# A two-layer hybrid encoder on one core: unread state products left out, and six loads of each feed-forward block given a place in the queue

## The chip, the cores and the metric

The kernel runs on one NeuronCore of a Trainium2 chip, as one program with one launch. The metric is the device time of that program in microseconds (us), lower is better. Five engines work beside each other, each from a queue of its own in a fixed order: TensorE (PE in the profile; its weight loads are PEld) multiplies matrices, VectorE (DVE) and ScalarE (ACT) work on elements, GpSimd (POOL) does some of that and issues DMAs, and SyncE (SP) issues most DMAs. All DMAs run on 16 shared DMA engines.

## The reference

The input is `x` (1024 tokens of 1024 values) and a memory of 256 tokens. `DEPTH` is 2, so there are two layers. Layer 0 mixes tokens with windowed attention, layer 1 with a two-directional gated recurrence; each mixer also has four cross-attention heads into the memory. Each layer ends with a feed-forward block. Cut to what matters here:

```python
h = x
for layer in range(2):
    u = rmsnorm(h, norm_g[layer, 0])
    y = mixer(u)                                   # 0: window attention, 1: recurrence
    h = h + rmsnorm(y, norm_g[layer, 1])
    f = conv_ffn(rmsnorm(h, norm_g[layer, 2]))     # gelu(conv(v @ w_gate)) * (v @ w_up) @ w_out
    h = h + rmsnorm(f, norm_g[layer, 3])

def step(state, inp):                              # the recurrence, one chunk of tokens
    qd, ke, vc, dec = inp
    o = qd @ state                                 # what earlier chunks give to this one
    state = dec * state + ke.T @ vc                # the state that the next chunk reads
    return state, o
```

The scan starts from a zero state and runs once over the tokens and once over the reversed tokens. The state after the last chunk of either scan is returned by the scan and used by nobody. The last `rmsnorm` of a layer has the weight `norm_g[layer, 3]`, and the first one of the next layer has `norm_g[layer + 1, 0]`.

## The kernel before

All products are float32 accurate: each operand is split into a high and a low part (`wh`, `wl`; `uh`, `ul`), and TensorE does three passes, high by high, high by low, low by high. The split is an ACT cast (L86, L76, L599) and a DVE subtraction (L87, L77, L600). The queues of all engines are written by a planner: it goes through the program with a model of the durations and puts each instruction into its engine's queue when, by its plan, the operands and a free buffer are there. A load with a free buffer therefore goes out as early as its buffer exists, however far back in the program it stands. `tc.issue_after(ins)` adds one rule: what is traced in the block on the engine of `ins` stands behind `ins` in that queue; it does not wait for `ins` to finish.

**The feed-forward block, `ffn(l, ...)`.** Its second half multiplies the 22 hidden tiles with `ffn_w_out` by a seven-product scheme (two by two blocks, seven instead of eight products). `SECOND = (1, 6, 7, 4, 2, 5, 3)` is the order of the seven products, called k below; each runs over p = 0 to 10, so there are 77 units (k, p). `unit(k, p)` loads two halves of one staging tile `st`, the weights (L891, from the input, or from `w2s`, sums of weight blocks made earlier in DRAM) and the hidden values (L892, `hid`), 256 KB each, and splits them. Staging has four buffers, the ring of split operands four. `second_ahead()` keeps up to three units made ahead of the one that TensorE works on. One unit is 12 matmuls of 128x512 (L575).

Around the units stand these loads, all on SP:

- `grow` (L104): one row of `norm_g` copied to all 128 partitions, 512 KB: `g3`, and in layer 0 also `g0`. Half of `g3` is then negated by DVE (L922). GpSimd first uses `g3` in `scaled`, after product 4 (L958).
- `rows(b, t)` (L935): 128 tokens of `h1d`, the layer's residual, 512 KB. The first four are for the token half `ia`: in the program they stand inside product 5, at p = 1, 3, 5 and 7, as the last argument of `tail`. `tail` adds the normed result to the row (DVE, L946), and SP stores it (L950). The tile `x` has four buffers in layer 0 and two in layer 1.

**The recurrence, `hgrn()`.** Eight heads; for each, `head` calls `direction` for the two scans d and the two token halves b in the order (0, 0), (1, 1), (0, 1), (1, 0). One call covers four chunks of 128 tokens. It ends with: `ER *= k` (DVE, L1237), four transposes of `ER` (PE, L1247), a copy of them to `kT` (ACT, L1249), four products `pu` of `kT` with the values (PE, L1252), and then the states `S`, one after another: `nx` is the chunk that reads the new state, and

```python
                if not 0 <= nx < NT:
                    continue
```

leaves out the state that no chunk reads. Its transpose and product were done by then. Which chunk that is: the last of the forward scan (d = 0, b = 1, c = 3) and the first of the backward scan (d = 1, b = 0, c = 0), so two of the sixteen chunks of each head. Between the directions stand the projections of the same and the next head (L81 to L83, the bulk of TensorE's work here) and the cross-attention units.

Of the kernel before, what the change touches and what calls it, by code (L numbers as in the profile page):

```python
# [8 lines left out]
F32 = mybir.dt.float32  # L9
# [4 lines left out]
ALU = mybir.AluOpType  # L14
# [4 lines left out]
P = 128  # L19
T = 1024  # L20
D = 1024
NT = T // P
# [25 lines left out]
def build(tc, A, out):  # L48
    nc = tc.nc
    act, dve, pool, pe = nc.scalar, nc.vector, nc.gpsimd, nc.tensor  # L50
# [34 lines left out]
    def split(h, l, src):  # L85
        act.copy(h, src)  # L86
        dve.tensor_tensor(l, src, h.bitcast(F32), op=ALU.subtract)  # L87
# [14 lines left out]
    def grow(pl, src_row, name):  # L102
        g = pl.tile([P, D], F32, tag=name, bufs=1, name=name)
        nc.sync.dma_start(g, src_row.to_broadcast([P, D]))  # L104
        return g
# [327 lines left out]
    class Out:  # L433
# [66 lines left out]
        def rows(self, wp, t):  # L500
            x = wp.tile([P, D], F32, tag="x", bufs=2, name="x")
            nc.sync.dma_start(x, self.src[t * P:(t + 1) * P, :])
            return x
# [75 lines left out]
    def ffn(l, wo, dst, gnext, halves_, out_halves):  # L579
# [10 lines left out]
        i, j = halves_  # L590
# [6 lines left out]
        def nsplit(h, l_, src):  # L597

            act.activation(h, src, AF.Copy, scale=-1.0)  # L599
            dve.scalar_tensor_tensor(l_, src, -1.0, h.bitcast(F32), op0=ALU.mult, op1=ALU.subtract)  # L600
# [119 lines left out]
        hd = dram.tile([8, NP2, P, 512], F32, name=f"hid{l}")  # L720
# [162 lines left out]
        SECOND = (1, 6, 7, 4, 2, 5, 3)  # L883
        where = {1: (2, None), 2: (3, None), 4: (1, None), 5: (None, 0), 7: (None, 1), 6: (None, 2), 3: (None, 3)}
        todo = [(k, p) for k in SECOND for p in range(NP2)]
        made = []

        def unit(k, p):
            r = stg.tile([P, 2, 512], F32, tag="st", name="st")
            a_, d_ = where[k]  # L890
            nc.sync.dma_start(r[:, 0, :], A["ffw2"][l, p, a_] if d_ is None else w2d[p][d_])  # L891
            nc.sync.dma_start(r[:, 1, :], hd[k, p])  # L892
            pl = hold_pool if k == 3 and 0 <= p - (NP2 - LAST[l]) < HOLD[l] else ring
            h, l_ = [pl.tile([P, 1024], F32R, tag=t, name=t) for t in ("wh", "wl")]
            r = r.rearrange("p a b -> p (a b)")
            if k == 6:
                nsplit(h[:, :512], l_[:, :512], r[:, :512])
                split(h[:, 512:], l_[:, 512:], r[:, 512:])
            else:
                split(h, l_, r)  # L900
            return h, l_

        def second_ahead():
            if todo and len(made) < (LAST[l] if todo[0][0] == 3 else 3):
                made.append(unit(*todo.pop(0)))
# [10 lines left out]
        np_ = tc.alloc_tile_pool(name=f"fn{l}", bufs=2, reuse_waits="tile")  # L916
        hold_pool = tc.alloc_tile_pool(name=f"fh{l}", bufs=HOLD[l], reuse_waits="tile")
        if gnext:
            tc.keep_in_program_order(act.preload_act_table_set("natural_log_exp_and_others"))
        g3 = grow(np_, A["norm_g"][l, 3:4, :], "g3")  # L920
        g0 = grow(np_, A["norm_g"][l + 1, 0:1, :], "g0") if gnext else None
        dve.tensor_scalar_mul(g3[:, 512:], g3[:, 512:], -1.0)  # L922
        y = {q: yp.tile([P, 4, 512], F32, name=q) for q in ("c11", "c21", "c12", "c22")}
        ss = {q: yp.tile([P, 4], F32, name=q) for q in ("q11", "q21", "q22")}
        left = lambda: {t: psl.tile([P, 512], F32, tag=f"x{t}", name="X") for t in (2, 3, 0, 1)}
# [3 lines left out]
        def rows(b, t):  # L929

            if gnext or b == ia:
                x = np_.tile([P, D], F32, tag="x", bufs=4 if gnext else 2, name="x")
            else:
                x = stg.tile([P, D], F32, tag="st", name="st")
            nc.sync.dma_start(x, h1d[l][tok(b, t), :])  # L935
            return x

        def tail(b, t, ya, sa, yb, sb, x):

            ts_ = tok(b, t)  # L940
            sq = np_.tile([P, 1], F32, tag="sq", name="sq")
            dve.tensor_tensor(sq, sa, sb, op=ALU.add)
            rs = rstd_of(np_, sq, 1, D, "p")
            last = not gnext and b == out_halves[1] and t == 3
            for c, yy in ((slice(0, 512), ya), (slice(512, 1024), yb)):
                dve.scalar_tensor_tensor(x[:, c], yy, rs[:, 0:1], x[:, c], op0=ALU.mult, op1=ALU.add)  # L946
                if last:
                    (nc.sync if c.start == 0 else act).dma_start(dst[ts_, c], x[:, c])
            if not last:
                nc.sync.dma_start(dst[ts_, :], x)  # L950
            if gnext:
                norm_T(np_, pst, x, g0, uh, ul, 4 * b + t)
# [12 lines left out]
        ia, ib = out_halves  # L965
        D0, D1 = slice(0, 512), slice(512, 1024)
        pst = None
        for k in SECOND:
            if k == 5:
                Xs = left()  # L970
            ps = Vs if k == 2 else Xs
            hold = []
            for p in range(NP2):
                while len(made) < 1:
                    second_ahead()
                h, l_ = made.pop(0)
                second_ahead()
                if k == 3 and p >= NP2 - LAST[l]:
                    hold.append((p, h, l_))
                else:  # L980
                    mms(k, p, h, l_, ps, range(4), k in (1, 5, 2) and p == 0)
                if k == 5 and p in (1, 3, 5, 7):
                    t = p // 2
                    tail(ia, t, y["c11"][:, t, :], ss["q11"][:, t:t + 1], y["c21"][:, t, :], ss["q21"][:, t:t + 1], rows(ia, t))
            if k == 3:
                last = [rows(ib, t) for t in range(4)]
            for t in range(4):
                if k in (1, 6, 7, 4):
                    act.copy(y[{1: "c11", 6: "c12", 7: "c22", 4: "c21"}[k]][:, t, :], ps[t])  # L989
                elif k in (2, 5):  # L990
                    q = y[{2: "c11", 5: "c22"}[k]][:, t, :]
                    dve.tensor_tensor(q, ps[t], q, op=ALU.add)  # L992
                else:
                    for p, h, l_ in hold:
                        mms(k, p, h, l_, ps, (t,), False)
                    sb = np_.tile([P, 1], F32, tag="sb", bufs=1, name="sb")
                    y1 = np_.tile([P, 512], F32, tag="y1", name="y1")
                    dve.tensor_tensor(y1, ps[t], y["c12"][:, t, :], op=ALU.add)  # L998
                    sumsq(np_, y1, sb)
                    y2 = np_.tile([P, 512], F32, tag="y2", bufs=1, name="y2")  # L1000
                    dve.tensor_tensor(y2, y1, g3[:, D0], op=ALU.mult)
                    tail(ib, t, y2, sb, y["c22"][:, t, :], ss["q22"][:, t:t + 1], last[t])
            if k == 4:
                scaled("c21", "q21", D1)
            elif k == 5:
                scaled("c22", "q22", D1)
            elif k == 2:
                scaled("c11", "q11", D0)
                psr.release()
                if gnext:  # L1010
                    pst = tc.alloc_tile_pool(name=f"fnps{l}", bufs=2, space=PSUM, side="right", reuse_waits="tile")
# [8 lines left out]
    def hgrn():  # L1020
        l = 1
        eq = tc.alloc_tile_pool(name="hgq", bufs=1, reuse_waits="tile")
        es = tc.alloc_tile_pool(name="hgs", bufs=1, reuse_waits="tile")
        early = tc.alloc_tile_pool(name="hg0", bufs=1, reuse_waits="tile")
# [126 lines left out]
        def direction(h, r, d, b, qin, S, As):  # L1151

            q, k = r["q"][b], r["s"][d][b]
# [25 lines left out]
            ER = early.tile([P, 512], F32, tag="ER", bufs=2, name="ER")  # L1179
# [54 lines left out]
            pool.tensor_copy(dec.unsqueeze(2), EP.rearrange("p (c t) -> p c t", t=P)[:, :, e:e + 1])  # L1234
            bs = slice(b * 512, (b + 1) * 512)
            sum_steps[1].send(pool.tensor_tensor(qin[:, bs], EP, q, op=ALU.mult))
            dve.tensor_tensor(ER, ER, k, op=ALU.mult)  # L1237
            dve.copy_predicated(Az[d], gm[d], pa.rearrange("p c t -> p (c t)"))
            a2 = lambda x: x.rearrange("p c t -> p (c t)")
            if As[b] is None:  # L1240
# [2 lines left out]
            else:  # L1243
                pool.tensor_tensor(a2(As[b]), a2(As[b]), Az[d], op=ALU.add)
            tp = bank("pt")
            for c in range(4):
                pe.transpose(tp[:, c, :], ER[:, c * P:(c + 1) * P], ident)  # L1247
            kT = wp.tile([P, 4, P], F32, tag="kT", bufs=1, name="kT")
            act.copy(kT, tp)  # L1249
            pu = bank("pu")  # L1250
            for c in range(4):
                pe.matmul(pu[:, c, :], kT[:, c, :], r["v"][:, 4 * b + c, :], start=True, stop=True)  # L1252
            for c in (range(3, -1, -1) if d else range(4)):
                cg = 4 * b + c
                nx = cg - 1 if d else cg + 1
                if not 0 <= nx < NT:
                    continue
                if cg == (NT - 1 if d else 0):
                    act.copy(S[:, nx, :], pu[:, c, :])
                else:  # L1260
                    dve.scalar_tensor_tensor(S[:, nx, :], S[:, cg, :], dec[:, c:c + 1], pu[:, c, :],
                                             op0=ALU.mult, op1=ALU.add)
# [300 lines left out]
```

## Time and profile before

| | before |
|---|---|
| median of 3 runs | 2662.06 us (2660.34 to 2668.28) |
| profiled execution, first to last instruction | 2663.0 us; the page gives no other time for it |
| PE busy | 2605.1 us, 98% |
| DVE, ACT, POOL busy | 1820.8 us, 1377.3 us, 468.3 us |
| second half of layer 0's feed-forward block, from its first jam of loads to its last unit | about 1005 to 1215 us |
| the recurrence | about 1245 to 1905 us |
| second half of layer 1's feed-forward block | about 2440 to 2660 us |

Matmuls overlap in these records: a 128x512 one is shown with 0.39 us, while the next one starts 0.227 us after it. How long a stretch of TensorE's work takes is therefore read from the starts, not from the durations. In the views in windows the columns after the engines are the granted TensorE clock (1.00 is full speed), the busy share of the DMA engines, and GB/s.

### The profile page before, as it was taken

What the parts mean: (1) busy time and instruction counts of PE and PEld (TensorE: products, weight loads), DVE (VectorE), ACT (ScalarE), POOL (GpSimd) and SP (SyncE); (2) the same over time, 40 slices, a digit from 0 to 9 for tenths busy, and PEclk for the clock granted to TensorE, in tenths of its full rate; (3) what the DMA queues carried; (4) which work ended last, traced back from release to release, by engine and by line L of the source; (5) the groups of instructions that cost most, each with busy time, mean ns of one, the idle gap of its engine ahead of it and who ended that gap; (6) DMA issues with size and microseconds to landing.
All of it is one profiled execution on the core that took longest, in us unless ns stands there. A gap on an engine that the chain in (4) does not pass through costs nothing. (4 is left out here: it accounts for less than half of the span.)

```text
span 2663.0 us, 39112 instructions
## 1 busy us (share of the span) xinstructions
PE 2605.1 (98%) x14420; PEld 2186.3 (82%) x14420; DVE 1820.8 (68%) x3043; ACT 1377.3 (52%) x2503; POOL 468.3 (18%) x520
## 2 busy tenths in 40 slices
PE   8999999999999999999999999999999999999998
PEld 7888887788888887887888888888887788888887
DVE  6778886578655565478688686887757755656447
ACT  6467676545444444455455554555534444444453
POOL 0321010211111100031224131231311111110013
PEclk9999999999999999999999999999999999999999
DMA  9772222367787857574235351103437778785666
GB/s 354 248 169 58 74 89 82 104 188 196 197 203 192 209 153 250 190 246 160 85 110 147 83 127 55 52 25 101 139 103 198 191 194 209 197 204 167 220 194 233
DMA packets 195728, 425.93 MB, mean 160 GB/s; under 512 B 20048, under 2 KB 56272, under 8 KB 189904
## 3 DMA queue, kind: packets, MB, share of 16 engines
q1 hardware_dynamic: 161552, 324.06, 37.6%
q0 software_dynamic: 24544, 90.19, 16.3%
q10 hardware_dynamic: 9440, 9.19, 1.1%
q8 instruction: 113, 1.85, 0.3%
q14 instruction: 79, 0.65, 0.1%
HBM read 330.04 MB, written 116.39 MB: 168 GB/s over the span
## 5 line engine op out<-in xcount | busy, mean ns | idle before, releaser
L87 DVE TENSOR_TENSOR wl<-st,wh 128x1024 fp32r<-128x1024 f32 (+1 forms) x238 | 263.4, 1113 | 318.4 <-ACT wh L86 308.1
L86 ACT CAST wh<-st 128x1024 fp32r<-128x1024 f32 (+1 forms) x238 | 222.5, 937 | 289.7 <-PE X L575 187.8
L81 PE MATMUL pj<-uh,wh 128*128 128x512 f32 x512 | 202.9, 397 | 4.0 <-DVE q L1118 2.0
L575 PE MATMUL X<-wl,wh 128*128 128x512 f32 x528 | 205.4, 391 | 0.3 <-DVE wl L87 0.3
L575 PE MATMUL X<-wh,wl 128*128 128x512 f32 x528 | 205.0, 390 | 0.0
L575 PE MATMUL X<-wh 128*128 128x512 f32 x528 | 199.6, 391 | 2.6 <-ACT c L989 2.1
L82 PE MATMUL pj<-ul,wh 128*128 128x512 f32 x512 | 201.7, 394 | 0.1
L83 PE MATMUL pj<-uh,wl 128*128 128x512 f32 x512 | 201.8, 394 | 0.0
L81 PE MATMUL pj<-wh,uh 128*128 128x384 f32 (+1 forms) x512 | 190.3, 373 | 4.7 <-DVE gs L1104 2.5
L83 PE MATMUL pj<-wh,ul 128*128 128x384 f32 (+1 forms) x512 | 187.7, 367 | 0.0
L82 PE MATMUL pj<-wl,uh 128*128 128x384 f32 (+1 forms) x512 | 187.3, 366 | 0.1
L77 DVE TENSOR_TENSOR wl<-st,wh 128x1024 fp32r<-128x1024 f32 (+1 forms) x91 | 116.3, 1283 | 26.0 <-ACT wh L76 25.3
L575 PE MATMUL V<-uh,wh 128*128 128x512 f32 x336 | 130.7, 389 | 0.0
L575 PE MATMUL V<-ul,wh 128*128 128x512 f32 x336 | 130.7, 389 | 0.0
L575 PE MATMUL V<-uh,wl 128*128 128x512 f32 x336 | 130.7, 389 | 0.0
L76 ACT CAST wh<-st 128x1024 fp32r<-128x1024 f32 (+1 forms) x97 | 97.7, 1013 | 44.9 <-PE pj L82 25.2
L575 PEld LDWEIGHTS X<-wh 128*128 128x128 f32 x528 | 99.5, 188 | 24.1 <-ACT c L989 2.5
L575 PEld LDWEIGHTS X<-wl,wh 128*128 128x128 f32 x528 | 99.6, 189 | 21.3 <-DVE wl L87 0.7
L575 PEld LDWEIGHTS X<-wh,wl 128*128 128x128 f32 x528 | 99.5, 188 | 20.7
L81 PEld LDWEIGHTS pj<-uh,wh 128*128 128x128 f32 x512 | 96.3, 188 | 24.2 <-DVE q L1118 3.1
L83 PEld LDWEIGHTS pj<-uh,wl 128*128 128x128 f32 x512 | 96.2, 188 | 18.6
L82 PEld LDWEIGHTS pj<-ul,wh 128*128 128x128 f32 x512 | 96.3, 188 | 18.6 <-DVE ul L87 0.4
(413 smaller groups left out, 7167.9 us busy)
## 6 DMA issues: line engine op xcount, KB each, us to landing
st<-hid SPq DMA_DIRECT2D x154, 256.0 KB, 3.0
st<-in_ffw_dram SPq DMA_DIRECT2D x108, 256.0 KB, 3.4
w2s<-in_ffw_dram POOLq DMA_DIRECT2D x24, 1024.0 KB, 8.4
st<-in_ffw_dram SPq DMA_DIRECT2D x46, 512.0 KB, 4.3
hid<-tt SPq DMA_DIRECT2D x88, 256.0 KB, 4.7
st<-w2s SPq DMA_DIRECT2D x88, 256.0 KB, 3.4
sx<-in_ffw_dram SPq DMA_DIRECT2D x84, 256.0 KB, 4.0
sy<-in_ffw_dram SPq DMA_DIRECT2D x42, 512.0 KB, 6.6
```

Of the source, the lines that this page charges most:

```text
L76: act.copy(h[:, :n], raw)
L77: (eng or dve).tensor_tensor(l[:, :n], raw, h[:, :n].bitcast(F32), op=ALU.subtract)
L81: pe.matmul(o, ah, bh, start=first, stop=False)
L82: pe.matmul(o, ah, bl, start=False, stop=False)
L83: return pe.matmul(o, al, bh, start=False, stop=last)
L86: act.copy(h, src)
L87: dve.tensor_tensor(l, src, h.bitcast(F32), op=ALU.subtract)
L575: last = pe.matmul(o, x, y, start=new, stop=e, skip_group_check=not first)
```

## The change

Two edits. In `direction`, only the chunks whose state is read (`used`, three of four in the two calls above) are multiplied, transposed, copied and multiplied with the values. In `ffn`, the tiles of `g3` and `g0` are still made at the head of the second half, but their loads are issued by `gain(0)` and `gain(1)` behind the hidden-value loads of units (7, 2) and (7, 6), and the rows 0 to 3 of the half `ia` behind those of units (4, 5), (4, 8), (5, 0) and (5, 3).

```diff
@@ unit @@
-            nc.sync.dma_start(r[:, 1, :], hd[k, p])
+            loads[k, p] = nc.sync.dma_start(r[:, 1, :], hd[k, p])
@@ ffn, head of the second half @@
-        g3 = grow(np_, A["norm_g"][l, 3:4, :], "g3")
-        g0 = grow(np_, A["norm_g"][l + 1, 0:1, :], "g0") if gnext else None
-        dve.tensor_scalar_mul(g3[:, 512:], g3[:, 512:], -1.0)
+        gains = [np_.tile([P, D], F32, tag=x, bufs=1, name=x) for x in (("g3", "g0") if gnext else ("g3",))]
+        g3, g0 = gains[0], gains[-1]
+
+        def gain(i):
+
+            nc.sync.dma_start(gains[i], A["norm_g"][l + i, 3 * (1 - i):3 * (1 - i) + 1, :].to_broadcast([P, D]))
+            if i == 0:
+                dve.tensor_scalar_mul(g3[:, 512:], g3[:, 512:], -1.0)
@@ ffn, the units @@
+        due, early = ([(4, 5), (4, 8), (5, 0), (5, 3)], [])
...
                 h, l_ = made.pop(0)
                 second_ahead()
+                if k == 7 and p in (2, 6) and p // 4 < len(gains):
+                    with tc.issue_after(loads[k, p].ins):
+                        gain(p // 4)
+                if k in (4, 5) and (k, p) in due:
+                    with tc.issue_after(loads[k, p].ins):
+                        early.append(rows(ia, due.index((k, p))))
...
-                    tail(ia, t, y["c11"][:, t, :], ss["q11"][:, t:t + 1], y["c21"][:, t, :], ss["q21"][:, t:t + 1], rows(ia, t))
+                    tail(ia, t, y["c11"][:, t, :], ss["q11"][:, t:t + 1], y["c21"][:, t, :], ss["q21"][:, t:t + 1], early[t])
@@ direction @@
-            dve.tensor_tensor(ER, ER, k, op=ALU.mult)
+            used = [c for c in range(4) if 4 * b + c != (0 if d else NT - 1)]
+            us_ = slice(used[0] * P, (used[-1] + 1) * P)
+            dve.tensor_tensor(ER[:, us_], ER[:, us_], k[:, us_], op=ALU.mult)
...
-            for c in range(4):
+            for c in used:
                 pe.transpose(tp[:, c, :], ER[:, c * P:(c + 1) * P], ident)
             kT = wp.tile([P, 4, P], F32, tag="kT", bufs=1, name="kT")
-            act.copy(kT, tp)
+            cs_ = slice(used[0], used[-1] + 1)
+            act.copy(kT[:, cs_], tp[:, cs_])
             pu = bank("pu")
-            for c in range(4):
+            for c in used:
                 pe.matmul(pu[:, c, :], kT[:, c, :], r["v"][:, 4 * b + c, :], start=True, stop=True)
-            for c in (range(3, -1, -1) if d else range(4)):
+            for c in (used[::-1] if d else used):
                 cg = 4 * b + c
                 nx = cg - 1 if d else cg + 1
-                if not 0 <= nx < NT:
-                    continue
```

More of the change, by code (lines that the diff above doesn't have):

```diff
@@ L885, in ffn @@
         todo = [(k, p) for k in SECOND for p in range(NP2)]
-        made = []
+        made, loads = [], {}
         def unit(k, p):
```

## The prediction, as written before the change was run

> **What bounds the kernel now.** I read the page's busy shares first, then windows over the stages, then TensorE's timeline wherever a window showed lost time, and last SP's queue and the waits at that place.
>
> ```profile
> span 2663.0 us, 39112 instructions
> PE 2605.1 (98%) x14420; PEld 2186.3 (82%) x14420; DVE 1820.8 (68%) x3043; ACT 1377.3 (52%) x2503; POOL 468.3 (18%) x520
> ```
>
> TensorE is busy for 98% of the span, so only two things shorten the run: less work for TensorE, or less of the 2663.0 − 2605.1 = 58 us of idling and slow clock. The change has one part of each kind. Windows over the second half of layer 0's feed-forward block (columns: time of PE, PEld, DVE, ACT, POOL, then clock, DMA share, GB/s):
>
> ```profile
> 1014.00:1024.00 10.00, 10.00 (x46) 8.29 (x45) 3.44 (x4) 3.43 (x4) 0.00 (x0) 1.00 1.00 356
> 1024.00:1034.00 10.00, 7.88 (x33) 6.16 (x32) 4.17 (x7) 4.75 (x10) 0.00 (x0) 0.93 0.97 373
> 1034.00:1044.00 10.00, 10.00 (x42) 8.19 (x41) 4.27 (x8) 4.72 (x9) 0.00 (x0) 0.90 0.34 113
> 1054.00:1064.00 10.00, 10.00 (x46) 8.29 (x45) 4.97 (x5) 5.07 (x8) 0.00 (x0) 1.00 0.63 204
> ```
>
> A usual stretch is the last one: 46 matmuls in 10 us, DMA engines 63% busy at 204 GB/s. From 1014 to 1034 the DMA engines are full, then TensorE gets only 33 and 42 matmuls, at a granted clock of 0.93 and 0.90. TensorE's timeline there, and two short windows:
>
> ```profile
> 1029.57 0.39 PE L575 MATMUL X<-wh 128*128 128x512 f32 x1
> 1029.80 0.39 PE L575 MATMUL X<-wl,wh 128*128 128x512 f32 x1
> 1030.02 0.39 PE L575 MATMUL X<-wh,wl 128*128 128x512 f32 x1
> 1032.53 0.80 PE L575 MATMUL X<-wh 128*128 128x512 f32 x1 [2.12 <-ACT c L989]
> ...
> 1036.03 0.39 PE L575 MATMUL X<-wh,wl 128*128 128x512 f32 x1
> ...
> 1032.00:1034.00 2.00, 1.47 (x4) 1.19 (x5) 1.18 (x2) 2.00 (x6) 0.00 (x0) 0.63 0.65 239
> 1034.00:1036.00 2.00, 2.00 (x6) 1.61 (x5) 1.19 (x3) 1.49 (x3) 0.00 (x0) 0.52 0.25 83
> ```
>
> Undisturbed, a matmul starts 0.22 to 0.23 us after the one before it; I use 0.227. The step from 1030.02 to 1032.53 is 2.51, so 2.28 us are lost waiting. The next 8 matmuls take 1036.03 − 1032.53 = 3.50 instead of 1.82 us, because the clock is about half: 1.68 lost. Together **4.0 us**. Who is late stands in SP's queue and in the waits between 1010 and 1035 (total, times, longest):
>
> ```profile
> 1013.67 0.95 SPq L104 DMA_DIRECT2D g<-in_norm_g_dram  x2
> 1015.65 1.18 SPq L935 DMA_DIRECT2D x<-h1d  x2
> 1021.82 1.51 SPq L935 DMA_DIRECT2D x<-h1d  x2
> ...
> ACT wh L599 <- DMA st<-w2s: 8.4, 3, 3.1
> DVE g L922 <- DMA g<-in_norm_g_dram: 5.3, 1, 5.3
> ```
>
> Both norm weights and four rows go out within 9 us, 6 x 512 KB = 3.15 MB, among the loads of the first units of product 6. ACT then waits three times for those weights, and TensorE runs dry once. The record names ACT's copy at L989 as what TensorE waited for; that copy stood behind a cast that waited for its load.
>
> **The change part by part.**
>
> *Loads in layer 0.* At 356 to 373 GB/s, 3.15 MB are 8.6 us of full DMA; three units of look-ahead are 3 x 12 x 0.227 = 8.2 us, and cast and subtraction need part of it. So the burst is just too long, by about the 2.28 us seen. Alone, 0.52 MB delays a unit's load by 1.4 us, and each 2.72 us unit leaves 37% of the DMA time free, 1.0 us: two units take the backlog off again. The six new places are at least three units apart. So the stall goes and I take **−4.0 us**; ends: 0 (the stall only moves) and −4.0 (all that is lost here). The trace has a smaller case, layer 1, with one weight and two rows:
>
> ```profile
> 2458.40 0.41 SPq L104 DMA_DIRECT2D g<-in_norm_g_dram  x1
> ...
> 2459.84 1.39 SPq L935 DMA_DIRECT2D x<-h1d  x2
> ...
> 2457.00:2467.00 10.00, 10.00 (x46) 8.28 (x45) 4.69 (x5) 3.45 (x4) 0.00 (x0) 1.00 1.00 352
> 2467.00:2477.00 10.00, 10.00 (x46) 8.29 (x45) 5.24 (x9) 6.25 (x12) 0.00 (x0) 1.00 0.87 314
> ```
>
> Half the burst, 1.57 MB or 4.3 us of full DMA, with 46 matmuls in both windows: covered. In layer 1 the move is worth **0**; the cover is the same look-ahead.
>
> The rule in the Trainium skill's "TensorE: Matmul & The Clock Gate", section "Why this matters for your kernels", is to leave no idle gap over some 3 us, since a window of idling halves the clock. By that rule the 2.3 us gap here should not have touched the clock, the slow stretch would have another cause and stay, and the sum would lose 1.7 us; in the trace the clock falls in the very window in which the gap ends.
>
> *Are the late loads late for their readers?* Old places of the units they now follow, first readers of the rows, and landing times of these row loads:
>
> ```profile
> 1052.74 0.32 SPq L891 DMA_DIRECT2D st<-w2s  x1
> 1145.58 0.32 SPq L891 DMA_DIRECT2D st<-w2s  x1
> ...
> 1168.61 1.41 DVE L946 SCALAR_TENSOR_TENSOR x<-c,prs,x 128x512 f32<-128x512 f32 x2
> ...
> DMA to landing us min/median/max: 4.2/5.7/10.4
> ```
>
> By the count of loads in SP's queue, 1052.74 is unit (7, 2) and 1145.58 is (5, 3). The last row moves to about 1146 and is read at 1168.61: 23 us, more than the worst landing. `g3` is first read after product 4, later still. DVE's negation of `g3` blocks the subtractions behind it until the load lands: 5.3 us before, in the jam; after, at most that, and under 8.2 us of look-ahead. Cost 0. GpSimd's queue carries none of these loads.
>
> *Third and fourth row of layer 1.* Tile `x` has two buffers there, so these two still cannot start before a stored row is out, wherever the program asks for them:
>
> ```profile
> 2607.49 0.32 SPq L935 DMA_DIRECT2D x<-h1d  x1
> 2610.91 0.32 SPq L935 DMA_DIRECT2D x<-h1d  x1
> SPq L935 <- DMA out_dram<-x: 1.7, 2, 1.2
> PE X L575 <- DVE c L992: 0.5, 1, 0.5
> PE X L575 <- DVE wl L87: 0.3, 1, 0.3
> ```
>
> SP waits 1.7 us for the stores, the unit loads behind it are late, and TensorE loses 0.5 + 0.3 us around 2624 and 2636. The store is on SP too, so a load placed right behind it could hold SP for one landing, some 4 us; ends: −0.8 and +2; I take 0.
>
> *Recurrence.* Removed: 8 heads x 2 chunks = 16 transposes and 16 products; a product is two matmul instructions. Timeline of one place, two group rows (count, busy us, mean ns), and the stage's sum row:
>
> ```profile
> 1282.84 0.60 PE L1252 MATMUL pu<-v,kT 128*128 128x128 f32 x4
> 1283.28 0.60 PE L1247 MATMUL pt<-ident,ER 128*128 128x128 f32 x4
> 1283.72 0.39 PE L1252 MATMUL pu<-v,kT 128*128 128x128 f32 x2
> ...
> L1237 DVE TENSOR_TENSOR ER<-ER,s 128x512 f32<-128x512 f32 x32 | 21.8, 681 | 0.0
> L1249 ACT COPY kT<-pt 128x512 f32<-128x512 f32 x32 | 18.7, 584 | 2.2 <-PE pt L1247 2.2
> ...
> sum 660.00, PE 650.43 PEld 549.02 DVE 512.92 ACT 350.44 POOL 173.19; mean PE 92.92 PEld 78.43 DVE 73.27 ACT 50.06 POOL 24.74
> PE pa L1201 <- POOL E L1216: 2.7, 4, 1.6
> PE pj L81 <- DVE gs L1104: 2.5, 4, 0.8
> ```
>
> Four of either take 0.44 us from start to start, 0.11 each: 16 x (2 + 1) x 0.11 = 5.3 us of TensorE's time. DVE's product and ACT's copy shrink by a quarter 16 times, at most 16 x 0.17 = 2.7 and 16 x 0.15 = 2.3 us; TensorE covers both, so 0. How much of 5.3 comes through? TensorE is busy 650.43 of the stage's 660.00 us. Ends: 0 (each saving falls into a wait for another engine) and 5.3 + 9.6 (the waits vanish too). The stage is 98.5% busy, so I take 0.985 x 5.3 = **−5.2 us**.
>
> *Sum.* 2663.0 − 4.0 − 5.2 = 2653.8 for an execution like the profiled one. The median of the runs is 2662.06, 0.9 lower, so **2652.9 us** for the median.
>
> **The rivals.**
>
> *The clock dip is not the wait's doing* and shows up again: 2652.9 + 1.7 = 2654.6. For it, a wait as long at the start of layer 1's block left the clock at full speed; against it, the coincidence above.
>
> ```profile
> PE Y L575 <- ACT wh L76: 2.2, 1, 2.2
> ...
> 2022.00:2026.00 4.00, 2.78 (x11) 1.83 (x12) 3.59 (x6) 1.90 (x3) 0.00 (x0) 1.00 0.57 126
> ```
>
> *The mixer's part is absorbed.* TensorE reaches the block products (`pa`) or the next projection sooner and waits there longer; the last two rows above are such waits, 5.2 us together. If half to all of 5.3 is lost so: 2655.5 to 2658.1. Against it: 98.5% busy.
>
> *The loads do harm at their new places, or the stall moves.* Price 4.0, time 2656.9. Against it: slack of 1.0 us in each unit, and layer 1's free 1.57 MB. The Trainium skill's "DMA: Bandwidth & Descriptors", section "Rules for kernel authors", advises to issue a DMA early and wait late; by that rule holding these loads back gains nothing, which is this rival's time. The trace disagrees: issued early, they made the weights late.
>
> *Slower: the planner reorders the recurrence.* Shorter directions shift its plan, and TensorE's queue may hold the `pa` products too early, before GpSimd's E is ready. Now that costs 2.7 us at 4 of 32 directions, 0.68 each. At 13 more directions the whole gain of 9.2 is gone (2662); at all 32, 28 x 0.68 = 19 is added: 2672, slower by 0.4%. For it: PE's queue is fixed by a plan that knows no real landing times. Against it: only 3 of 4 steps shrink slightly, in half the calls.
>
> *Better than the sum.* DVE's 2.7 us come before TensorE's waits, and the stage's 9.6 us and layer 1's 0.8 us of waits shrink by half: 2648.
>
> **How the numbers follow.** Forecast 0.46; clock dip stays 0.08; mixer's part absorbed 0.15; loads do harm 0.11; planner 0.10, of it 0.07 beyond 2670; better 0.10. A measurement of this kernel tells about 0.3%, 8 us, from no change: faster means under 2654.1. The forecast has about 2.5 us of scatter from a rewritten plan, so 0.65 of its 0.46 lie below that (0.30), all of the better case (0.10), and 0.03 each of the clock and absorbed cases: faster 0.46, same 0.47, slower 0.07. The range takes in the better case's 2648 and, above, the absorbed and the harm cases with scatter, 2661; it leaves out the planner case and the better case's far side.
>
> **What would show it.** Right: full DMA windows around 1014 to 1034 gone, no wait of TensorE near 1030 and a clock of 1.00 there; weight and row loads one by one behind units of products 7, 4 and 5, the rows of layer 1 still near its end; 224 instead of 256 `pu` matmuls, 112 instead of 128 transposes, recurrence shorter by about 5 us. Wrong: longer waits of `pa` or `pj`, a new wait of TensorE after a moved load, or SP held longer at L935.

## The result, and the profile after

| | before | after |
|---|---|---|
| median of 7 runs each | 2662.06 us (2658.89 to 2668.28) | 2673.07 us (2669.26 to 2675.41) |
| ratio, 95% interval | | 1.0034 [1.0024, 1.0044] |
| profiled execution, span | 2663.0 us | 2673.6 us |

The kernel became 11 us slower; 9 us faster was forecast. The runs after give the time of an execution beside its span: 2675.33 for 2673.6, so some 1.75 us lie around the span. The head of the page of after:

```profile
span 2673.6 us, 39030 instructions
PE 2610.2 (98%) x14372; PEld 2186.9 (82%) x14372; DVE 1820.9 (68%) x3043; ACT 1374.7 (51%) x2503; POOL 465.8 (17%) x520
```

TensorE does 48 instructions less (14420 before) and is busy 5 us longer. Where the 10.6 us of span arise is read from stages, cut at instructions that both kernels have: the recurrence from its first to its last `pa` grew from 638.3 to 649.8 us (+11.5), the second half of layer 0's feed-forward block shrank by 3.3 us, the stages ahead of it took 2.3 us longer with nothing changed in them, and the rest agrees within 0.7 us each. So one edit did as told and the other the opposite.

*The feed-forward edit.* Windows over the old jam in after, and rows of SP's timeline:

```profile
1016.00:1026.00 10.00, 10.00 (x46) 8.26 (x44) 4.44 (x6) 4.31 (x5) 0.00 (x0) 1.00 0.84 275
1026.00:1036.00 10.00, 10.00 (x46) 8.29 (x45) 4.45 (x7) 5.39 (x10) 0.00 (x0) 1.00 0.60 198
```

```profile
1051.97 0.37 SPq L925 DMA_DIRECT2D g<-in_norm_g_dram  x1
1063.43 0.33 SPq L925 DMA_DIRECT2D g<-in_norm_g_dram  x1
1090.37 0.42 SPq L940 DMA_DIRECT2D x<-h1d  x1
...
2617.51 0.38 SPq L940 DMA_DIRECT2D x<-h1d  x1
```

46 matmuls in both windows, no slow clock, DMA engines no longer full; weights and rows go out one by one. The third row of layer 1 (2617.51) still stands near the end, 10 us later than before like everything there.

*The mixer's edit.* The work named is gone. Two group rows of after, both for the recurrence (count, then busy us and mean ns):

```profile
L1267 PE MATMUL pu<-v,kT 128*128 128x128 f32 x224 | 34.5, 280 | 0.9 <-ACT kT L1264 0.4 <-DVE v L1114 0.3
L1261 PE MATMUL pt<-ident,ER 128*128 128x128 f32 x112 | 18.5, 281 | 2.7 <-ACT ot L1319 2.7
```

Still the stage is longer. One window from first to last `pa`, in before and in after (columns as in the prediction: length, then PE, PEld, DVE, ACT and POOL, clock, DMA share, GB/s):

```profile
1260.70:1899.00 638.30, 629.63 (x5078) 531.90 (x5079) 494.24 (x977) 338.06 (x731) 167.87 (x177) 1.00 0.31 88
```

```profile
1259.40:1909.20 649.80, 634.32 (x5035) 532.84 (x5035) 494.59 (x977) 335.36 (x731) 164.09 (x177) 0.98 0.31 86
```

TensorE has 43 recorded matmuls less, yet 4.7 us more busy time, at a clock of 0.98, and idles 15.5 instead of 8.7 us. Its waits there in after (total, times, longest), and two windows in which the clock fell:

```profile
PE pj L81 <- DVE gs L1116: 5.8, 4, 3.9
PE pa L1213 <- POOL E L1228: 3.2, 3, 2.0
PE pj L81 <- DVE q L1130: 2.7, 1, 2.7
PE pt L1261 <- ACT ot L1319: 2.7, 1, 2.7
...
1343.00:1443.00 100.00, 93.36 (x767) 78.81 (x766) 79.91 (x164) 49.94 (x118) 33.81 (x39) 0.95 0.38 125
1543.00:1643.00 100.00, 94.73 (x805) 78.89 (x804) 80.69 (x161) 49.40 (x107) 34.02 (x35) 0.95 0.41 94
```

Four waits are long: 2.7 us (for `q`, at 1383), 3.9 (`gs`, 1433), 2.7 (`ot`, 1552) and 2.0 (E, 1606), 11.3 together. A clock of 0.95 over 100 us is 10 us at half speed, so both windows hold 20 us of that and lose 10. The timeline of after at the first place:

```profile
1377.60 0.62 ACT L1256 COPY As<-Az 128x512 f32<-128x512 f32 x1
1381.27 0.69 ACT L1319 ACTIVATE ot<-pt,bng 128x512 f32<-128x512 f32 x1 [3.05 <-DMA oT<-ot]
1381.86 0.59 ACT L1092 ACTIVATE q<-pj 128x512 f32<-128x512 f32 x1
...
1384.51 0.62 ACT L1094 ACTIVATE q<-q 128x512 f32<-128x512 f32 x1
...
1385.65 0.68 DVE L1130 TENSOR_TENSOR q<-pj,q 128x512 f32<-128x512 f32 x1
...
1386.39 0.50 PE L81 MATMUL pj<-uh,wh 128*128 128x512 f32 x1 [2.72 <-DVE q L1130]
```

and ACT's timeline of before at the same work:

```profile
1374.60 0.69 ACT L1306 ACTIVATE ot<-pt,bng 128x512 f32<-128x512 f32 x1
...
1378.92 0.60 ACT L1080 ACTIVATE q<-pj 128x512 f32<-128x512 f32 x1
...
1381.97 0.67 ACT L1306 ACTIVATE ot<-pt,bng 128x512 f32<-128x512 f32 x1
```

`ot`, a head's finished output, has one buffer, so its next copy needs the store of the last one out. Before, the first step of `q`'s sigmoid stood ahead of the second `ot` copy, and the copy did not wait. After, the copy stands ahead: ACT, which works in order, waits 3.05 us for the store, `q` is late, the bank `pj` is not free, and TensorE stands still. No instruction of this place was removed: the copies to `kT` on either side (1377.13 and 1385.17) are whole ones of 128x512. The other three places in after:

```profile
1436.55 0.41 DVE L1116 TENSOR_TENSOR gs<-pj,gs 128x256 f32<-128x256 f32 x1
1437.11 0.77 PE L81 MATMUL pj<-wh,uh 128*128 128x512 f32 x1 [3.92 <-DVE gs L1116]
...
1551.48 0.62 ACT L194 CAST kvh<-kvl 128x512 fp32r<-128x512 f32 x1 [4.98 <-DMA kvl<-kvd]
...
1555.62 1.11 PE L1261 MATMUL pt<-ident,ER 128*128 128x128 f32 x4 [2.68 <-ACT ot L1319]
...
1606.06 0.76 POOL L1228 TENSOR_TENSOR E<-EP,q 128x256 f32<-128x256 f32 x1 [2.04 <-DVE EP L1221]
1608.60 1.12 PE L1213 MATMUL pa<-E 128*32 128x64 f32 x59 [2.01 <-POOL E L1228]
```

At 1552 ACT has waited 4.98 us for a load of the cross-attention; at 1433 DVE is late; only at 1606 do the `pa` products stand ahead of GpSimd's E.

Set against before instruction by instruction, the mixer's edit alone puts some 160 VectorE, 90 ScalarE and 300 TensorE instructions (beside the 32 removed) elsewhere in the queues; the feed-forward edit alone 2, 1 and 6.

### The profile page after: what moved, and what is told of

Read it like the earlier page. It is cut to its first block, busy times and chain, and to the rows that moved or that the text cites. A ratio compares the mean times of both kernels' runs of the same rounds, so it can differ in the third digit from the quotient of the medians.

```text
span 2673.6 us, 39030 instructions
## 1 busy us (share of the span) xinstructions
PE 2610.2 (98%) x14372; PEld 2186.9 (82%) x14372; DVE 1820.9 (68%) x3043; ACT 1374.7 (51%) x2503; POOL 465.8 (17%) x520
## 5 line engine op out<-in xcount | busy, mean ns | idle before, releaser
L81 PEld LDWEIGHTS pj<-wh,uh 128*128 128x128 f32 x512 | 97.1, 190 | 20.1 <-issue 4.3
```

What stands on the lines that cost most here:

```text
L81: pe.matmul(o, ah, bh, start=first, stop=False)
```

## The experiments

Theory: the planner's new order of the recurrence costs the time, not the edits. Rivals: the feed-forward edit has a part in it; the missing work itself opens the gaps. Times are medians, with ratios to runs of before on the same chip.

**The edits one by one, and with the order held.** The first two kernels are the hunks of the diff by themselves. In the other two the queues of TensorE, VectorE and ScalarE within the recurrence are held to before's order, without the 32 instructions, by edges that fix only the order of issue:

```diff
+    def pin(made):
+        for eng, steps in PINNED.items():      # positions of before's queue, as differences
...
+                if last is not None:
+                    tc.add_manual_dep(mine[at], last.name, mybir.DependencyInfo(
+                        mybir.DependencyClass.NoSync, mybir.DependencyReason.DATA), reason="pinned")
+                last = mine[at]
...
+    seen = len(nc.cur_bb.bb.instructions)
     late = hgrn()
+    pin([i for i in nc.cur_bb.bb.instructions[seen:] if "BassTile" not in type(i).__name__])
```

> The feed-forward edit alone; the recurrence as before. Plan theory (the mixer edit makes the planner write another order for the recurrence, and that order costs more than the left-out work saves; the loads do what was forecast): 4 us below the kernel before, about 2658, with no wait of TensorE near 1030 and the recurrence unchanged, first to last block product 638.3 us. Rival (the moved loads shift the state in which the recurrence's plan begins, and that shift makes the bad order): slower by 6 us or more, first to last block product about 650.

Measured: 2662.33 us, ratio 0.9997 [0.9988, 1.0006]; first to last `pa` 638.3 us, as before. TensorE no longer waits near 1030, but the 4 us expected of the loads do not show in the time. The feed-forward edit has no part in the loss.

> The mixer edit alone; the loads as before. Plan theory: about 15 us above e1, some 2673 to 2676: first to last block product about 650 instead of 638.3 us, waits of TensorE over 2 us at four places with half-clock windows behind them, and the 4.0 us stall near 1030 as in the kernel before. Rival (the two edits only hurt together): 5 us below the kernel before, 2657.

Measured: 2674.84 us, 1.0047 [1.0034, 1.0060]; first to last `pa` 650.1 us, with the same four waits (5.8, 3.2, 2.8, 2.6 us in total). The wait near 1030 was 1.1 us, with no slow clock behind it, and not the stall of 4.0 us that was expected. All of the loss is the mixer's edit's.

> The mixer edit alone, but TensorE's, VectorE's and ScalarE's queues in the recurrence are held by edges of issue order to the order of the kernel before, less the 32 left-out instructions. Plan theory: the saving comes out, 5.2 us below the kernel before, about 2657, first to last block product 633 us. Rival (the left-out work itself hurts, for instance since shorter bursts idle TensorE and halve its clock): slower, near e2.

Measured: 2660.45 us, 0.9990 [0.9981, 0.9999]. Window from first to last `pa` and the two largest waits of this kernel:

```profile
1258.00:1890.80 632.80, 624.65 (x5034) 526.83 (x5034) 490.91 (x977) 336.41 (x731) 165.99 (x177) 1.00 0.31 89
...
PE pa L1230 <- POOL E L1245: 3.6, 5, 1.6
PE pj L110 <- DVE gs L1133: 2.5, 4, 0.8
```

The same work in before's order takes 632.8 us, 5.5 less than before and 17 less than after. The median time fell by only 2.4 us against before on the same chip, not by the 5.2 expected; its eleven executions lie between 2655.91 and 2662.60 us, and the stage is read from one of them, of 2657.43. Of the 17, 9.7 are TensorE's busy time (634.32 against 624.65, with as many matmuls: the half clock) and 7.3 its idle time.

> Both edits, with the recurrence's three queues held to the order of the kernel before as in e3. Plan theory: 9.2 us below the kernel before, about 2653, the time that was forecast. Rival (either part was worth nothing): 2657 to 2662.

Measured: 2657.40 us, 0.9981 [0.9972, 0.9989]; first to last `pa` 633.9 us. Both edits with the order held beat both kernels. The gain against before on the same chip is 5.4 us, not 9.2, and the time alone lies inside the rival's range; the stage, 4.5 us shorter, speaks against the rival for the recurrence's part.

**The order alone.** All the work of before in the order of the mixer's edit: this keeps the order and takes the missing work away as a cause.

```diff
 # before, nothing removed
+PINNED: the queues of the kernel with the mixer's edit, the 32 put back beside their neighbours
```

> All the work of the kernel before (the 32 unread transposes and products are computed), with the orders of TensorE, VectorE and ScalarE in the recurrence held to those of the kernel with the mixer's edit alone; each of the 32 stands beside its neighbour chunk. Theory A (the order alone costs the time): first to last pa = 650 of the mixer's edit + 5.3 for the 32 = about 655 us (652 to 658), the time 2662.5 + 17 = about 2679 (2675 to 2683), and the four long waits of TensorE near 1383, 1432, 1552 and 1606 come back within a few us of those places. Theory B (the order is harmless by itself, the missing work is what opens gaps on TensorE, and these bring the half clock): with the work back the gaps are filled, first to last pa is about 638 (636 to 641), the time about 2662.

Measured: 2672.42 us, 1.0033 [1.0021, 1.0045]. Window and waits:

```profile
1256.20:1909.70 653.50, 636.94 (x5081) 536.37 (x5080) 495.94 (x977) 337.31 (x731) 166.84 (x177) 0.99 0.30 86
...
PE pj L112 <- DVE gs L1135: 5.7, 4, 3.9
PE pj L112 <- DVE q L1149: 3.9, 3, 3.1
PE pt L1278 <- ACT ot L1337: 3.3, 1, 3.3
```

Theory A: 653.5 us against 655 expected, and the long waits are back, at 1381, 1432, 1552 and 1607, with no work missing. The time came out 3 us under its range of 2675 to 2683, though the stage was within its own.

**How small an edit is enough.** One chunk of 16 left out, as a difference to the mixer's edit:

```diff
-            used = [c for c in range(4) if 4 * b + c != (0 if d else NT - 1)]
+            used = [c for c in range(4) if not ((h,d)==(1,0)) or 4 * b + c != (0 if d else NT - 1)]
```

> Of the mixer's edit only one chunk of 16 is left out: that of head 1, scan 0 (one transpose and one product fewer, one copy and one VectorE product narrower); all else is computed as before and the planner writes the order: 95 VectorE, 45 ScalarE and 155 further TensorE instructions change places. Theory A (the order costs the time): the recurrence moves by much more than the work left out, by 2 us or more (first to last pa 640 to 650 if the new order is as bad as that of the full edit; a lucky order could be as far below, 630 to 636). Theory B (time follows the work left out): 0.33 us less, first to last pa 637.5 to 638.5, the time within 0.1% of before.

Measured: 2675.91 us, 1.0046 [1.0029, 1.0063].

```profile
1258.20:1908.10 649.90, 635.05 (x5076) 535.33 (x5076) 494.75 (x977) 336.07 (x731) 170.71 (x177) 0.99 0.30 86
...
PE pj L81 <- DVE q L1118: 5.2, 2, 4.3
```

A third of a microsecond of work less costs 11.6 us of the stage, as much as all 16 chunks, in other places (1549 and 1601). Then the same kernel with TensorE's order held:

> The one chunk of head 1, scan 0 left out as in the run of one chunk (649.9 us first to last pa, the time 2675.9), now with TensorE's order held to that of the kernel before without that one transpose and product. Theory (the order alone is the cause): first to last pa 637.5 to 638.5, the time 2661 to 2663, no wait of 2.6 us or more. Rival (the narrower product and copy shift VectorE's and ScalarE's results so that TensorE waits whatever its own order): 641 or more, the time above 2665.

Measured: 2665.00 us, 1.0008 [0.9998, 1.0017]; first to last `pa` 639.9 us, clock 1.00, and no step of TensorE over 1.9 us there. The order brings 10 of the 11.6 us back; the last 1.6 are spread over short waits, and neither prediction had them. What moves them is open.

**Which queue.** The mixer's edit with the order of one engine held, the others left to the planner.

> The mixer's whole edit with ScalarE's order alone held to that of the kernel before; the planner writes the others (VectorE 86 and TensorE 276 beside the 32 in other places). Theory A1 (ScalarE's order does the harm: at 1383 and 1552 a copy or cast at its head waited for a transfer and held what stood behind it): those two waits go, first to last pa 633 to 638, the time 2659 to 2664. Theory A2 (VectorE's and TensorE's order does it): first to last pa 643 to 650, the time 2667 to 2675.

Measured: 2674.44 us, 1.0036 [1.0023, 1.0049].

```profile
1257.60:1907.70 650.10, 632.45 (x5042) 533.87 (x5043) 488.01 (x977) 334.41 (x731) 165.51 (x177) 0.99 0.30 86
...
PE pa L1213 <- POOL E L1228: 7.3, 4, 2.6
PE pt L1302 <- DVE on L1298: 6.1, 3, 3.1
```

Nothing is won: the waits for `ot` and `q` shrink to 1.6 and 0.9 us, as theory A1 said, but others for E and `on` come, in the new order of TensorE and VectorE that the planner wrote this time. Holding ScalarE's order is not enough; whether it caused the two waits in the first place is not shown.

> The mixer's whole edit with TensorE's order alone held to that of the kernel before without the 32; the planner writes VectorE's and ScalarE's (31 and 8 instructions in other places, against 160 and 87 for the edit with no order held). Theory A2 (TensorE's order, and with it VectorE's, does the harm): first to last pa 632 to 636, the time 2658 to 2662, as with all three held. Theory A1 (ScalarE's does it): the same if its 8 moves are not those, otherwise 638 to 645.

Measured: 2658.22 us, 0.9981 [0.9972, 0.9990].

```profile
1255.40:1887.50 632.10, 624.71 (x5035) 526.99 (x5034) 491.62 (x977) 335.56 (x731) 166.45 (x176) 1.00 0.31 89
...
PE pa L1217 <- POOL E L1232: 2.9, 4, 1.6
```

With TensorE's order alone held, the planner puts nearly all of the rest back by itself. The stage has its full gain, 6.2 us; the time is 4.2 us below before on the same chip.

> All the work of the kernel before, with TensorE's order alone held to that of the kernel with the mixer's edit (each of the 32 beside its neighbour chunk); the planner writes the other queues. Theory A2 (TensorE's order is enough to lose the time, the planner fits the others to it): first to last pa 650 to 656, the time 2670 to 2680. Theory A3 (it needs the other queues' order as well): 638 to 645, the time 2662 to 2668.

Measured: 2671.68 us, 1.0035 [1.0024, 1.0046].

```profile
1256.80:1905.20 648.40, 633.99 (x5081) 533.95 (x5080) 494.81 (x977) 337.35 (x731) 166.58 (x177) 0.99 0.31 87
...
PE pj L98 <- DVE gs L1121: 5.8, 4, 3.9
PE pt L1264 <- ACT ot L1323: 3.5, 1, 3.5
```

The reverse: TensorE's new order alone, with all work done, loses 10.1 of the 15.2 us that all three new orders lose; the waits for `gs`, `ot` and E are back, the one for `q` is not. The stage fell between the two expectations.

> The mixer's whole edit with VectorE's order alone held to that of the kernel before; the planner writes the others (ScalarE 52 and TensorE 156 beside the 32 in other places). Theory A2 (TensorE's order decides): with 156 of TensorE's instructions still in new places part of the loss stays, first to last pa 638 to 650, the time 2663 to 2675. Theory A4 (VectorE's order decides, and TensorE's only follows it): 632 to 636, the time 2658 to 2662.

Measured: 2669.20 us, 1.0024 [1.0012, 1.0035].

```profile
1257.40:1903.00 645.60, 630.20 (x5038) 530.37 (x5039) 490.32 (x977) 336.11 (x732) 168.26 (x177) 0.99 0.31 87
```

With VectorE's order held and 156 of TensorE's instructions in new places, 13 of the 17 us stay. Of the three orders TensorE's weighs most: held alone, it keeps the gain or brings two thirds of the loss. In either run the planner fitted the other two queues to it almost wholly (all but 31 VectorE and 8 ScalarE instructions to before's order in the one, all but some 35 and 6 to that of the mixer's edit in the other, by the order in the traces), so no run here shows TensorE's order at work with the others unchanged.

**The best version.**

> Both edits, with TensorE's order in the recurrence alone held to that of the kernel before without the 32. Theory (TensorE's order decides, the feed-forward edit adds its own small part): first to last pa 631.5 to 634.5, no wait of TensorE over 2 us and no half clock window in the recurrence, second half of layer 0's second pass 212.9 to 213.6 against 214.2 to 215.1 where the loads were not moved; time 2656 to 2658 (2658.2 with the mixer's edit and this order, less the 1 to 2 us of the wait for c). Rival (the edits do not add up: the moved loads cost elsewhere what the wait brought): 2658 to 2660.

Measured: 2656.64 us, 0.9979 [0.9969, 0.9989]; first to last `pa` 632.5 us, the second half of layer 0's block 212.9 us. This is the fastest kernel, though not told apart from the one with all three queues held, nor from the mixer's edit alone with TensorE's held (0.9981).

## Why the prediction was wrong

*The term for the recurrence, −5.2, right in size, lost to another.* With the order kept, the stage shrank by 5.5 (all three held), 4.5 (the same with both edits), 6.2 (TensorE held) and 5.8 us (the same with both edits). The working (48 short matmul instructions, 0.11 us each, TensorE full) stands. The step that failed is the sum around it: it added up removed instructions on queues taken as unchanged otherwise, and so put the planner's new order at nothing, while front and prediction both said that a planner writes the queues. The new order cost 17 us with the edit in, and 15.2 with no work removed.

*The rival "the planner reorders the recurrence" was the outcome, with a wrong place and too low a chance.* It expected up to 28 further waits of 0.68 us at the `pa` products. Waits for E rose only from 2.7 to 3.2 us in total. The time went into four long waits at four different releasers, and over half of it into the clock that fell behind them, which that rival had not priced. Its end, 2672 us, was met by chance. Its "against", that only 3 of 4 steps shrink slightly, held its chance at 0.10, and was wrong: a single chunk left out moves 95 VectorE instructions and costs 11.6 us.

*The feed-forward term, −4.0, was about −1.4.* The mechanism was right: the burst is gone, and so is the wait. The size came from one execution. The wait of TensorE for `c` near 1030 is 2.1 us in before's profile, but in the nine kernels whose loads were not moved it lies between 0.5 and 1.9 us. The one of the order-held mixer's edit, with its window:

```profile
PE X L604 <- ACT c L1018: 1.9, 1, 1.9
...
1024.00:1034.00 10.00, 8.10 (x36) 6.40 (x35) 3.82 (x6) 4.78 (x10) 0.00 (x0) 1.00 0.91 354
1034.00:1044.00 10.00, 10.00 (x46) 8.29 (x45) 5.16 (x9) 4.98 (x10) 0.00 (x0) 1.00 0.56 178
```

Full DMA, a wait, and the clock stays at 1.00: in none of the nine did it fall there. So the 1.68 us of half clock were no regular part of the stall. They were the wait's doing all the same, and not another cause's as one rival had it: the last section shows when a wait costs clock. The wait at the start of layer 1's block, to which that rival pointed, was cut in before's execution into 1.5 and 0.9 us by the border between two slots of the grid described there. From first to last unit this half takes 212.9 to 213.6 us with the edit and 214.4 (median of the nine) without: 1.4 us. Timed alone the edit gives nothing that can be told from no change (0.9997); between the two kernels with three queues held it gives 3 us, between the two with TensorE's held less than 2, and in both pairs the intervals overlap. That it is worth 1.4 us is thus read from the stage of single executions, not from the time.

*The step from the profiled execution to the median took off the dip where it probably was not.* The profiled execution's time was about 2663.0 + 1.75 = 2664.8 us, 2.7 above the median and not 0.9. The forecast is in effect the median less 9.2, and 1.7 of the 9.2 are a dip of this one execution, which none of the nine other traces with unmoved loads has; that the median execution lacks it is likely, not shown.

*What held.* Layer 1's move was worth 0, its two late rows still wait for the stores, as said, and no moved load held TensorE up: between 1040 and 1245 it waits 0.9 us in all in after, VectorE 3.0 us for `g`, within the 5.3 allowed. By the terms as measured, 5.5 and 1.4, the change was worth 6.9 us in before's order; the two held versions measured 5.4 and 6.0. The mixer's edit alone, held, measured 2.4 and 4.2 us in time against 5.5 and 6.2 in the stage; where the rest went is open.

## What to carry to other kernels

Where a scheduler writes the queues, a removed instruction has two prices: its own duration, and that of the order written anew around it. Compare the order of the queues first, and if more than the edited instructions moved, give no sum of durations any weight; hold the old order of the bounding engine (here TensorE alone was enough) and then measure the edit. A loss that one profiled execution shows is priced from several, above all where the clock has a part in it.

## What the runs showed of the hardware

The clock fell behind waits shorter than expected, and not always. In the recurrences all 18 steps of TensorE of 2.6 us or more from one matmul's start to the next were followed by a stretch at half clock; of the nine steps between 2.0 and 2.6 in the recurrences and near 1030, four were. The equal step of 2.43 us at the start of layer 1's block stands in all 14 kernels and cost clock in six.

The clock records in the traces show what decides. Within an execution all stretches at half clock begin on one grid of slots of 3.413 us and last one slot or two: in after they begin at 336.34, 418.26, 1387.65, 1435.43, 1554.90, 1609.51 and 2032.77 us, which are 24, 284, 14, 35, 16 and 124 slots apart. Where the grid lies differs from one execution to the next. What counts is how long TensorE idles (no matmul of it runs, by its records) within one slot. Two slots at the start of layer 1's block, each with the slot behind it, in the one-chunk kernel with TensorE held and in the kernel with ScalarE held:

```profile
2021.39:2024.80 3.41, 1.04 (x4) 0.55 (x4) 3.41 (x5) 3.11 (x5) 0.00 (x0) 1.00 0.27 86
2024.80:2028.21 3.41, 3.41 (x9) 2.58 (x9) 1.38 (x2) 0.00 (x0) 0.00 (x0) 0.50 0.74 225
...
2027.39:2030.81 3.42, 1.50 (x11) 1.12 (x9) 2.19 (x4) 2.80 (x6) 0.54 (x1) 1.00 0.31 126
2030.81:2034.22 3.41, 2.96 (x11) 2.01 (x12) 2.82 (x4) 1.14 (x2) 0.00 (x0) 1.00 0.62 151
```

It is the same step of 2.43 us. In the first kernel 2.37 us of idling lie in one slot, and the next slot runs at half clock; in the second the slot's end cuts the idling into 1.9 and 0.5, and the clock stays. Between 1000 and 2640 us of the 14 traces, all 27 slots at full clock with 1.95 us of idling or more were followed by half clock, three of the ten with 1.75 to 1.91, and none with less. In the first 430 us some slots with 1.3 to 1.8 us were followed by it too, so idling as these records show it is not the whole rule.

The Trainium skill's "TensorE: Matmul & The Clock Gate" gives two rules: in "Why this matters for your kernels" no idle gap over some 3 us, in Part 1 a window of 3413 ns that runs freely. The first would have left the 2.0 us wait at 1606 and the 2.1 us wait near 1030 alone, and the trace disagrees; the grid of 3.413 us agrees with the second. A stretch cost about 1.7 us, near half of the 3.4 us that it lasted, or twice that.
